# A two-layer float32 decoder trunk: six of eight MLP up-projection groups computed as 2x2 Strassen block products

## The chip, the core and the metric

The kernel runs on one core of a Trainium2 chip. The metric is the device time of one execution in microseconds (us). Five engines run their own instruction queues in order and wait for each other through semaphores: TensorE (PE in the profile, its weight loads as PEld), VectorE (DVE), ScalarE (ACT), GpSimd (POOL) and SyncE (SP), which here issues the DMA loads. Matmuls write PSUM, everything else lives in SBUF.

## The reference, cut to what matters

One sequence of 256 rows and 1024 columns goes through two layers. Each layer adds a normed mixer (retention in layer 0, block attention in layer 1) and then a normed MLP of width 4096:

```
def sq_relu_mlp(x, w_up, w_down):
    h = jax.nn.relu(x @ w_up)
    return (h * h) @ w_down
...
    h = h + rms_norm(mixers[i % N_MIXERS](rms_norm(h, pre), w_in, w_out), post)
    h = h + rms_norm(sq_relu_mlp(rms_norm(h, mpre), w_up, w_down), mpost)
```

All of it is float32. The change touches `x @ w_up` alone, 256 x 1024 times 1024 x 4096, once in each layer.

## The kernel before, in words

**Split products.** A float32 operand is split into two float32r parts, `hi` (a ScalarE copy) and `lo` (VectorE: operand minus `hi`). A product is three matmuls into one PSUM bank: hi*hi, hi*lo, lo*hi (`mm`, L178 to L180). The 256 rows are two row tiles of 128 (`t`); the 1024 inner columns are eight k tiles.

**Weight stream.** `Stream` brings weights as chunks of 128 x 1024 (512 KB). SP loads a chunk into one of four `raw` buffers, ScalarE writes `whi` (L134), VectorE `wlo` (L135). At most ten split chunks are live (`slots`); one is given back when its last matmul has been issued. `used` counts that down.

**Order of emission.** One Python program writes all queues. `Flow.now` is a clock that `mm` moves on by the planned time of its matmuls; side chains (generators such as `act_rows`) say after how much planned time they go on, and `pump` splits the next chunk when the planned time `next_t` has come and the chunk's load is planned to have landed. The order so made is the order in each engine's queue. On the chip nothing is reordered.

**The MLP** (`mlp`). The hidden width 4096 is eight groups of 512 columns.

- Groups 0 and 1 (`in_groups_skewed`): activations are the stationary operand, 512 weight columns the moving one. Row tile 0 of both groups comes first, then row tile 1. Each result goes through `act_rows`: ScalarE relu (`r`), VectorE square (`sq`), four TensorE transposes (`turn4`, tile `tp_u`), and a split of the transposed tile by ScalarE and VectorE into `hid[g]`.
- Groups 2 to 7 (`up_cols`): 128 weight columns are stationary and all 256 rows move, so results (`upc`) come out transposed and no `turn4` is needed. A group takes 4 column tiles x 8 k tiles x 3 = 96 matmuls of 256 columns. `act_cols` is relu, square, split.
- After each such group come four steps of the down projection (`step_out`, tile `dn`), each 2 row tiles x 2 column halves x 3 matmuls of 512 columns. In layer 1 the last of the four accumulators is kept as two tiles of 256 columns, so the end of the kernel can start on the first half (`finish_last`).

SP issues every load; GpSimd does only small work. In front of the MLP the function `post` finishes the mixer: norm, residual into `h`, transposition (`tp_h`), gain (`hg`), split, and a ScalarE pass over `h` for the next row norm (`pre_stats`).

Of the kernel before, what the change touches and what calls it, by code (L numbers as in the profile page):

```python
# [84 lines left out]
class Chunk:  # L85
    def __init__(self, hi, lo):
        self.hi, self.lo, self.left = hi, lo, CH * S


class Stream:  # L90
    """Weight chunks in the order of use: loaded, then split into two float32r parts."""

    def __init__(self, tc, ctx, flow, slots, raws):
        self.nc = tc.nc
        self.pool = ctx.enter_context(tc.tile_pool(name="wst", bufs=1))
        self.flow, self.slots, self.raws = flow, slots, raws
        self.src, self.raw, self.ready = [], [], []
        self.live, self.next_t, self.dma_t = 0, 0.0, 0.0
        flow.pump = self.pump

    def load(self):
        """issue the next chunk's load, and the other loads that come before it"""
        while self.src:
            s = self.src.pop(0)
            self.dma_t = max(self.dma_t, self.flow.now + 1.6)
            if callable(s):
                s()
                self.dma_t += 1.0
                continue
# [10 lines left out]
            return  # L120

    def split(self, pres=(None,)):
        nc = self.nc
        if not self.raw:
            self.load()
        raw = self.raw.pop(0)[0]
        hi = self.pool.tile([P, CH], F32R, tag="whi", name="whi", bufs=self.slots)
        lo = self.pool.tile([P, CH], F32R, tag="wlo", name="wlo", bufs=self.slots)
        n = len(pres)
# [7 lines left out]
        self.ready.append(Chunk(hi, lo))  # L137
        self.next_t = max(self.next_t, self.flow.now) + (1.3 if len(self.ready) < 4 else 2.0)
        while len(self.raw) < self.raws and self.src:
            self.load()  # L140

    def pump(self):
        while self.live < self.slots and self.flow.now >= self.next_t:
            if not self.raw:
                self.load()
            if not self.raw or self.flow.now < self.raw[0][1]:
                return
            self.split()
# [14 lines left out]
def body(ctx, tc, xT, x, gT, gpost, w_in_0, w_out_0, w_up_0, w_down_0, w_in_1, w_out_1, w_up_1, w_down_1,  # L163
# [12 lines left out]
    def mm(o, a, b, first, last):  # L176
        """o += a.T @ b; a, b: (hi, lo) pairs of float32r parts."""
        nc.tensor.matmul(o, a[0], b[0], start=first, stop=False)  # L178
        nc.tensor.matmul(o, a[0], b[1], start=False, stop=False)  # L179
        nc.tensor.matmul(o, a[1], b[0], start=False, stop=last)  # L180
        flow.now += 3 * b[0].shape[-1] / 2400

    def mm_rows(o, a, w, s, first, last):
        """activations stationary: o [128 rows, columns s of w]"""
        mm(o, a, (w.hi[:, s], w.lo[:, s]), first, last)
# [4 lines left out]
    def mm_cols(o, w, s, b, first, last):  # L190
        """weights stationary: o [128 columns s of w, all rows]"""
# [44 lines left out]
    h = [cpool.tile([P, D], F32, name=f"h{t}") for t in range(NT)]  # L236
    table = small_t("table")
    nc.scalar.activation(table, mhalf, AF.Copy)

    def rsqrt(ss):  # L240
        """(ss + eps) ** -0.5"""
# [6 lines left out]
    def pre_stats(t):  # L248
        """1 / rms of the rows of h[t]"""
# [4 lines left out]
    class HT:  # L254
        """h transposed, times the norm's gain, as two parts; its rows' 1 / rms come later."""
# [23 lines left out]
    class Post:  # L279
        """rms_norm of the rows z * sc, taken in parts as they come"""  # L280
# [8 lines left out]
        def part(self, z, c0):  # L289
            """the columns from c0"""  # L290
# [22 lines left out]
    def post(z, t, sc, gb, nxt, gi):  # L313
        """h[t] += rms_norm(z * sc) * gain; then h[t] transposed for the next layer."""
# [9 lines left out]
        hg = []  # L324
        for n in range(2):
            tp = new_ps([P, 4, P], "tp_h")
            turn4(tp, h[t][:, n * 512:(n + 1) * 512])
            hg.append(new_e2([P, 4, P], "hg"))
            gn = g_sb[:, gi, n * 4:n * 4 + 4]
            nc.vector.tensor_mul(hg[n], tp, gn[:, :, None].to_broadcast([P, 4, P]))  # L330
        yield 0.8
        for n in range(2):
            n4, ts = slice(n * 4, n * 4 + 4), slice(t * P, (t + 1) * P)
            split(nxt.hi[:, n4, ts], nxt.lo[:, n4, ts], hg[n])
# [11 lines left out]
    def finish_out(acc, lhs, k0, nk, sc, gb, nxt, gi):  # L346
        """the rest of an output projection and the norm after it, row tile 0 ahead of row tile 1"""
# [14 lines left out]
    def in_tile(hT, w, c, t, o):  # L362
        """two k tiles of one group of 512 columns"""
# [4 lines left out]
    def in_group_both(hT):  # L368
        """one group of 512 columns for both row tiles, chunk after chunk"""
# [7 lines left out]
    def in_groups_skewed(hT, then):  # L377
        """two groups of 512 columns, row tile 0 ahead of row tile 1"""
# [9 lines left out]
        hT.ready(1)  # L388
        for g in range(2):
# [6 lines left out]
    def mlp(hT, gain, nxt, gi):  # L396
# [18 lines left out]
        def act_cols(g, jp, o):  # L415
            r = new_e2([P, 2, S], "r")
            nc.scalar.activation(r, o, AF.Relu)  # L417
            sq = new_e2([P, 2, S], "sq")
            nc.vector.tensor_mul(sq, r, r)
            yield 0.8  # L420
            j2 = slice(jp * 2, jp * 2 + 2)
            split(hid[g][:, 0, j2, :], hid[g][:, 1, j2, :], sq)

        def up_cols(g):
            chunks = [ws.get() for _ in range(4)]
            for jp in range(2):
                o = new_ps([P, 2, S], "upc")
                for j in range(2):
                    f0 = (jp * 2 + j) * P
                    for k in range(KD):  # L430
                        s = slice((k % 2) * 512 + f0, (k % 2) * 512 + f0 + P)
                        mm_cols(o[:, j, :], chunks[k // 2], s, hT.both(k), k == 0, k == KD - 1)
                done[g].append(flow.spawn(act_cols(g, jp, o)))
# [8 lines left out]
        in_groups_skewed(hT, lambda g, t, o: done[g].append(flow.spawn(act_rows(g, t, o))))  # L442
# [10 lines left out]
        for g in range(2, NG):  # L453
            new_hid(g)
            up_cols(g)
            for k in range((g - 2) * 4, (g - 1) * 4):
                w = ws.get()
                for t in range(NT):
                    step_out(acc, lhs, k, t, w, nk)
# [55 lines left out]
    def load_h(t):  # L515
        return lambda: nc.sync.dma_start(h[t], x[t * P:(t + 1) * P, :])

    src = ws.src
    wi = [w_in_0[c] for c in range(48)]
    src += [(wi[0], (load_x(0, 1), load_x(1, 1))), (wi[1], (load_x(2, 2), None)), (wi[2], (load_x(4, 2), None)), load_x(6, 2),  # L520
            wi[3], wi[4], wi[5], wi[6], wi[7], load_h(0), load_h(1), lambda: nc.sync.dma_start(csr, cs0), wi[8],
            load_decay(0), wi[9], wi[10], wi[11]]
    for hd in range(1, RH):
        src += wi[hd * 12:hd * 12 + 6] + [load_decay(hd)] + wi[hd * 12 + 6:hd * 12 + 12]
        if hd == 1:
            src += [lambda: consts.update(gb=load_gain(0))]
    src += [w_out_0[k] for k in range(16)]

    def mlp_order(up, down):
        o = [up[c] for c in range(8)]  # L530
        for g in range(2, NG):
            o += [up[g * 4 + c] for c in range(4)]
            o += [down[(g - 2) * 4 + c] for c in range(4)]
        return o + [down[(NG - 2) * 4 + c] for c in range(8)]

    src += mlp_order(w_up_0, w_down_0)
    src += [w_in_1[g * 4 + c] for g in (0, 1, 3, 4, 2, 5) for c in range(4)]
    src += [w_out_1[k] for k in range(MH)]
    src += mlp_order(w_up_1, w_down_1)
# [9 lines left out]
    def qk_tile(o, i, c, w):  # L549
        """two k tiles of one of the four 128-column tiles of a head's q and k (even, odd)"""  # L550
# [4 lines left out]
    def first_stats():  # L555
        """1 / rms of the rows of x, also into the rotary tables"""
# [130 lines left out]
    hT = mlp(hT, 1, HT, 2)  # L687

# [11 lines left out]
    def prep(qk, u, t, ps, wait):  # L700
        """rotary and transposition of q or k of four heads, one row tile"""
# [24 lines left out]
    def softmax(qk, pall, hp, t, *after):  # L726
        """rows of softmax(q k.T) of two heads, one row tile; b is the weight of a key out of reach"""
# [34 lines left out]
    def turn(pall, pts, after):  # L762
        """the probabilities transposed, head after head"""
# [32 lines left out]
    def pts_of(a, b):  # L796
        """two tiles of 2048 columns -> the parts of four heads' transposed probabilities"""
# [17 lines left out]
    def heads0(qk, pq):  # L815
        """the first four heads: all that follows their q and k"""
# [11 lines left out]
    def heads1(qk, pq):  # L828
        """the last four heads, up to their transposed probabilities"""
# [43 lines left out]
    mlp(hT, 3, None, None)  # L873
# [4 lines left out]
def _groups(w, cols):  # L878
    """[K, N] -> chunks of [128, 2 x 512]: groups of 512 columns in the order cols, two k tiles a chunk"""
# [3 lines left out]
    return w.reshape(n * 4, P, CH)  # L883

# [63 lines left out]
```

## Time and profile before

| | us |
|---|---|
| device time, 3 runs: median (lowest to highest) | 690.31 (690.25 to 691.45) |
| profiled execution: span, first to last instruction | 688.4 |
| median run less that span (the profile gives no other total of its own) | 1.9 |
| PE busy, share of span | 676.1 (98%) |
| DVE busy, share | 419.4 (61%) |
| ACT busy, share | 350.4 (51%) |
| POOL busy, share | 82.2 (12%) |
[...]

Busy times are of instructions that overlap in a pipelined engine: the length of one matmul in the profile (0.39 us for 512 columns) is not the step between two matmuls. That step is read from two start times in the timeline. "Releaser" is the instruction that ended an engine's wait.

### The profile page before, as it was taken

To read this page: it belongs to the slowest core of one execution; us is meant where nothing else is said; L and a number is where in the kernel's file an instruction comes from. 1 tells how busy PE (TensorE), PEld (TensorE's weight loads), DVE (VectorE), ACT (ScalarE), POOL (GpSimd) and SP (SyncE) were. 2 spreads that over 40 slices of the span, in tenths; PEclk is the share of its full clock that TensorE was granted. 3 is DMA by queue.
4 is the path that set the end of the run, shared out by engine and by line. 5 is a ranking of instruction groups with operands and counts; after the bars stand their busy time and mean duration, and the time that the engine had idled before them with its cause. 6 is when DMAs were issued, how large, how long until landed. Compare 5 with 4: busy or idle time off the path is not lost. (4 is left out here: it accounts for less than half of the span.)

```text
span 688.4 us, 10014 instructions
## 1 busy us (share of the span) xinstructions
PE 676.1 (98%) x3919; PEld 594.3 (86%) x3919; DVE 419.4 (61%) x521; ACT 350.4 (51%) x493; POOL 82.2 (12%) x138
## 2 busy tenths in 40 slices
PE   8999999999999999999999999999999999999996
PEld 6889898988888988998898878888889999999985
DVE  5669576656458665545653867867686654465513
ACT  6475555445346545435542657755465554345411
POOL 0222120201001000000000263922010000000001
PEclk9999999999999999999999999999999999999998
DMA  7767565464624774457545456543246744674401
GB/s 274 284 208 267 200 212 177 155 206 154 241 93 157 241 251 169 157 190 244 176 140 175 169 184 219 184 148 123 83 161 235 258 155 151 211 231 148 164 9 62
DMA packets 36191, 125.09 MB, mean 182 GB/s; under 512 B 4272, under 2 KB 4784, under 8 KB 36144
## 3 DMA queue, kind: packets, MB, share of 16 engines
q1 hardware_dynamic: 36144, 124.45, 53.0%
q8 instruction: 31, 0.51, 0.3%
q14 instruction: 16, 0.13, 0.1%
HBM read 123.39 MB, written 1.05 MB: 181 GB/s over the span
## 5 line engine op out<-in xcount | busy, mean ns | idle before, releaser
L135 DVE TENSOR_TENSOR wlo<-raw,whi 128x1024 fp32r<-128x1024 f32 (+1 forms) x227 | 271.5, 1212 | 114.1 <-ACT whi L134 112.8
L134 ACT ACTIVATE whi<-raw 128x1024 fp32r<-128x1024 f32 (+1 forms) x227 | 231.1, 1042 | 86.9 <-DMA raw<-in_w_down 21.1
L178 PE MATMUL ip<-whi,act 128*128 128x512 f32 x288 | 114.2, 397 | 0.0
L179 PE MATMUL ip<-wlo,act 128*128 128x512 f32 x288 | 112.5, 391 | 0.2 <-DVE wlo L135 0.2
L180 PE MATMUL ip<-whi,act 128*128 128x512 f32 x288 | 112.4, 390 | 0.0
L178 PE MATMUL upc<-act,whi 128*128 128x256 f32 x384 | 108.8, 283 | 0.0
L180 PE MATMUL upc<-act,wlo 128*128 128x256 f32 x384 | 108.7, 283 | 0.0
L179 PE MATMUL upc<-act,whi 128*128 128x256 f32 x384 | 108.7, 283 | 0.0
L179 PE MATMUL dn<-wlo,act 128*128 128x512 f32 (+1 forms) x288 | 105.6, 367 | 0.0
L178 PE MATMUL dn<-whi,act 128*128 128x512 f32 (+1 forms) x288 | 105.6, 367 | 0.0
L180 PE MATMUL dn<-whi,act 128*128 128x512 f32 (+1 forms) x288 | 105.3, 366 | 0.0
L178 PEld LDWEIGHTS upc<-act,whi 128*128 128x128 f32 x384 | 73.7, 192 | 0.3
L179 PEld LDWEIGHTS upc<-act,whi 128*128 128x128 f32 x384 | 73.7, 192 | 0.3
L180 PEld LDWEIGHTS upc<-act,wlo 128*128 128x128 f32 x384 | 73.7, 192 | 0.0
L180 PEld LDWEIGHTS ip<-whi,act 128*128 128x128 f32 x288 | 54.1, 188 | 11.6
L179 PEld LDWEIGHTS ip<-wlo,act 128*128 128x128 f32 x288 | 54.2, 188 | 10.7 <-DVE wlo L135 0.7
L178 PEld LDWEIGHTS ip<-whi,act 128*128 128x128 f32 x288 | 54.2, 188 | 10.0
L178 PEld LDWEIGHTS dn<-whi,act 128*128 128x128 f32 x288 | 54.4, 189 | 8.9
L180 PEld LDWEIGHTS dn<-whi,act 128*128 128x128 f32 x288 | 54.2, 188 | 8.9
L179 PEld LDWEIGHTS dn<-wlo,act 128*128 128x128 f32 x288 | 54.4, 189 | 8.6
L310 POOL TENSOR_TENSOR po_c<-po_sum,mhalf 128x1 f32<-128x1 f32 x8 | 4.5, 563 | 379.4 <-DVE po_sum L298 379.4
L417 ACT ACTIVATE r<-upc 128x512 f32<-128x512 f32 x24 | 14.3, 597 | 60.8 <-PE upc L180 60.8
(156 smaller groups left out, 862.4 us busy)
## 6 DMA issues: line engine op xcount, KB each, us to landing
raw<-in_w_in SPq DMA_DIRECT2D x69, 512.0 KB, 3.9
raw<-in_w_up SPq DMA_DIRECT2D x64, 512.0 KB, 4.5
raw<-in_w_down SPq DMA_DIRECT2D x64, 512.0 KB, 4.1
raw<-in_w_out SPq DMA_DIRECT2D x24, 512.0 KB, 3.3
gb<-in_gpost SPq DMA_DIRECT2D x4, 512.0 KB, 5.4
raw<-in_w_in SPq DMA_DIRECT2D x6, 256.0 KB, 5.6
h<-in_x SPq DMA_DIRECT2D x2, 512.0 KB, 6.6
dT_sb<-in_dT SPq DMA_DIRECT2D x4, 256.0 KB, 4.8
```

The lines of the kernel that those rows point to most:

```text
L134: nc.scalar.activation(hi[:, c], raw[:, c], AF.Copy)
L135: nc.vector.tensor_sub(lo[:, c], raw[:, c], hi[:, c].bitcast(F32))
L178: nc.tensor.matmul(o, a[0], b[0], start=first, stop=False)
L179: nc.tensor.matmul(o, a[0], b[1], start=False, stop=False)
L180: nc.tensor.matmul(o, a[1], b[0], start=False, stop=last)
L310: nc.gpsimd.tensor_tensor(c, self.ss, mhalf, ALU.pow)
L417: nc.scalar.activation(r, o, AF.Relu)
```

## The change

Groups 2 to 7 are taken in three pairs in each layer. A pair's up projection is a 2 x 2 block product: rows halve into the two row tiles, the inner 1024 into even and odd k tiles (each 4 tiles of 128), the 1024 columns of the pair into its two groups. Seven products of blocks (Winograd's form of Strassen's scheme) take the place of eight. Each product is 4 k tiles x 3 matmuls of 512 columns with activations, or a sum of activation blocks, as the stationary operand. The products go into three PSUM tiles, `px`, `py`, `pz`, some of them accumulated on top of an earlier one.

- **Activation sums**, once per MLP (`block_sums`): four sums of blocks of `hg`, each then split; eight VectorE and four ScalarE instructions of 128 x 512. `hg` now stays in SBUF for that.
- **Weight sums.** The up weights of a pair are loaded into four `quad` tiles of 128 x 2048, each in two halves. Two block sums are VectorE adds in place (`u1`, `u2`; L187), two are accumulating DMAs from SBUF to SBUF that GpSimd issues (`u3`, `u4`; L191). A pair has four VectorE adds and four such DMAs, 512 KB each.
- **Chunks.** A pair now splits 14 half blocks instead of 8 chunks of up weights, beside 8 chunks of down weights as before. A half block is used by 6 matmuls of 512 columns.
- **Results.** `squared` adds the stored blocks on VectorE (`c`, with `u2`, `u3`, `p1` as helpers), then ScalarE does relu and square, and after 1.6 planned us `turned` issues four transposes on TensorE and a split. A pair has four of these.
- **Order.** `up_blocks` alternates one product and one down step. `down()` is one step of 12 + 12 matmuls.
- **Pace.** While the quads are open a split costs the plan 1.5 us, an add 1.1 us, an accumulating DMA 2.8 us of the queue and 7.0 us to land.
- Layer 1's last accumulator is one tile of 512 columns again.

```
+    def product(o, lhsT, first):
+            for half in range(2):
+                w = ws.get()
+                for kk in range(2):
+                    kp = 2 * half + kk
+                    mm_rows(o, lhsT(kp), w, slice(kk * 512, (kk + 1) * 512), first and kp == 0, kp == 3,
+                            not first)
...
+    def up_blocks(g, down):
+            x = new_ps([P, 512], "px")
+            product(x, quad(0, 0), True)
+            p1 = new_e2([P, 512], "p1")
+            nc.scalar.activation(p1, x, AF.Copy)
+            down()
+            flow.finish(*sums)
+            z = new_ps([P, 512], "pz")
+            product(z, hsum(0), True)
+            down()
+            y = new_ps([P, 512], "py")
+            product(y, hsum(1), True)
+            u2 = new_e2([P, 512], "u2")
+            nc.vector.tensor_add(u2, y, p1)
+            down()
+            product(y, hsum(2), False)
+            u3 = new_e2([P, 512], "u3")
+            nc.vector.tensor_add(u3, y, p1)
+            squared(g + 1, 1, z, u3, -1.0)
+            down()
+            product(x, quad(0, 1), False)
+            squared(g, 0, x)
+            down()
+            product(y, quad(1, 1), False)
+            squared(g, 1, y, p1)
+            down()
+            product(z, hsum(3), False)
+            squared(g + 1, 0, z, u2, -1.0)
+            down()
+            down()
...
+        def squared(g, t, o, add=None, sign=1.0):
+            c = new_e2([P, 512], "c")
+            if add is None:
+                nc.scalar.activation(c, o, AF.Relu, scale=sign)
+            else:
+                nc.vector.tensor_add(c, o, add)
+                nc.scalar.activation(c, c, AF.Relu, scale=sign)
+            nc.scalar.activation(c, c, AF.Square)
+            done[g].append(flow.spawn(turned(g, t, c)))
...
+                if name[1] in ("u1", "u2"):
+                    nc.vector.tensor_add(o, o, a)
+                    cost += 1.1
+                    self.landed[name] = 0.0
+                else:
+                    nc.gpsimd.dma_start(o, a, accum_op=ALU.add)
+                    self.dma_t = max(self.dma_t, self.flow.now) + 2.8
+                    self.landed[name] = self.flow.now + 7.0
...
-        if nxt is None:
-            acc[1] = [acc[1][0], acc[1][1][:, :256], new_ps([P, 256], "dn4")]
```

**Place 1: VectorE, start of layer 0's MLP.** `sq` is the square of a result of groups 0 and 1, `act<-tp_u` the split of a transposed one, `rs_a` the end of `post`. Before, between the square of (group 0, row tile 0) and that of (group 0, row tile 1):

```order
L408 TENSOR_TENSOR sq<-r 128x512
L135 TENSOR_TENSOR wlo<-raw,whi 128x1024
L198 TENSOR_TENSOR act<-hg,act 128x4x128 x2
L135 TENSOR_TENSOR wlo<-raw,whi 128x1024
L198 TENSOR_TENSOR act<-tp_u,act 128x4x128
L243 TENSOR_SCALAR rs_a<-pre_ss 128x1
L408 TENSOR_TENSOR sq<-r 128x512
L135 TENSOR_TENSOR wlo<-raw,whi 128x1024 x2
L198 TENSOR_TENSOR act<-tp_u,act 128x4x128
L135 TENSOR_TENSOR wlo<-raw,whi 128x1024
L408 TENSOR_TENSOR sq<-r 128x512
```

The last row is the square of (group 0, row tile 1). Now, up to the same square; after `rs_a` and ahead of these rows stand five more: a split of `quad_2029`, an add into it, the square of (group 1, row tile 0), a block sum, a split of `quad_2029`:

```order
L187 TENSOR_TENSOR quad_2029<-quad_2029,quad_2030 128x1024
L505 SCALAR_TENSOR_TENSOR hsum<-hsum,hg 128x512
L258 TENSOR_TENSOR s_lo<-hsum,s_hi 128x512
L258 TENSOR_TENSOR act<-tp_u,act 128x4x128
L508 TENSOR_TENSOR hsum<-hg 128x512
L258 TENSOR_TENSOR s_lo<-hsum,s_hi 128x512
L182 TENSOR_TENSOR wlo<-raw,whi 128x1024
L182 TENSOR_TENSOR wlo<-quad_2029,whi 128x1024
L187 TENSOR_TENSOR quad_2029<-quad_2029,quad_2031 128x1024
L511 SCALAR_TENSOR_TENSOR hsum<-hsum,hg 128x512
L258 TENSOR_TENSOR s_lo<-hsum,s_hi 128x512
L470 TENSOR_TENSOR sq<-r 128x512
```

Behind `rs_a` that square was the sixth instruction. It is now the seventeenth: four splits of chunks, three adds, four block sums, three splits of sums, the split of a turned block and the square of (group 1, row tile 0) stand ahead of it.

**Place 2: VectorE, second half of a pair.** Layer 0, the pair of groups 4 and 5, from the split of the pair's second turned block (`act<-tp_u`) to the last `c`. `quad_2032` is the first block of the next pair. Before, one whole group there:

```order
L135 TENSOR_TENSOR wlo<-raw,whi 128x1024
L419 TENSOR_TENSOR sq<-r 128x512
L135 TENSOR_TENSOR wlo<-raw,whi 128x1024
L198 TENSOR_TENSOR act<-sq,act 128x512
L135 TENSOR_TENSOR wlo<-raw,whi 128x1024 x6
L419 TENSOR_TENSOR sq<-r 128x512
L198 TENSOR_TENSOR act<-sq,act 128x512
```

Now:

```order
L258 TENSOR_TENSOR act<-tp_u,act 128x4x128
L182 TENSOR_TENSOR wlo<-raw,whi 128x1024
L182 TENSOR_TENSOR wlo<-quad_2032,whi 128x1024
L187 TENSOR_TENSOR quad_2032<-quad_2032,quad_2031 128x1024
L491 TENSOR_TENSOR c<-py,p_2665 128x512
L258 TENSOR_TENSOR act<-tp_u,act 128x4x128
L182 TENSOR_TENSOR wlo<-quad_2032,whi 128x1024
L187 TENSOR_TENSOR quad_2032<-quad_2032,quad_2031 128x1024
L182 TENSOR_TENSOR wlo<-raw,whi 128x1024
L491 TENSOR_TENSOR c<-pz,u_2747 128x512
```

Two rows of the next pair's first block stand directly in front of `c<-py`, three rows of splitting and adding in front of `c<-pz`.

**Place 3: TensorE, layer 0, groups 2 and 3, from the end of the third `py` product.** Before, a down step (`dn`) was followed by the next down step or by the next group, with no transposes; two steps meet like this:

```order
L178 MATMUL dn_2255<-whi_2212,act_2027 128x512
L179 MATMUL dn_2255<-wlo_2213,act_2027 128x512
L180 MATMUL dn_2255<-whi_2212,act_2027 128x512
L178 MATMUL dn_2252<-whi_2234,act_2027 128x512
L179 MATMUL dn_2252<-wlo_2235,act_2027 128x512
```

Now (each accumulator `dn_` has three matmuls):

```order
L240 MATMUL py_2376<-whi_2423,act_1669 128x512
L238 MATMUL dn_2274<-whi_2442,act_2036 128x512
L239 MATMUL dn_2274<-wlo_2443,act_2036 128x512
L240 MATMUL dn_2274<-whi_2442,act_2036 128x512
L238 MATMUL dn_2275<-whi_2442,act_2036 128x512
L239 MATMUL dn_2275<-wlo_2443,act_2036 128x512
L240 MATMUL dn_2275<-whi_2442,act_2036 128x512
L238 MATMUL dn_2276<-whi_2442,act_2036 128x512
L239 MATMUL dn_2276<-wlo_2443,act_2036 128x512
L240 MATMUL dn_2276<-whi_2442,act_2036 128x512
L262 MATMUL tp_u_2555<-ident_96,c_2542 128x128 x4
L238 MATMUL dn_2277<-whi_2442,act_2036 128x512
```

The four transposes of `c` stand nine matmuls behind the product whose result `c` holds. It is so in all six pairs, four times in each.

## Rows read from the trace of the kernel before

**Rows 1.** The page: busy time of the engines, TensorE's granted clock in 40 slices.
```profile
PE 676.1 (98%) x3919; PEld 594.3 (86%) x3919; DVE 419.4 (61%) x521; ACT 350.4 (51%) x493; POOL 82.2 (12%) x138
...
PEclk9999999999999999999999999999999999999998
```
**Rows 2.** Windows, layer 1: length, busy PE, PEld, DVE, ACT, POOL, clock, DMA, GB/s.
```profile
580.85:603.49 22.64, 22.64 (x158) 21.14 (x157) 12.21 (x13) 10.38 (x12) 0.00 (x0) 1.00 0.58 186
603.49:626.13 22.64, 22.64 (x158) 21.14 (x157) 12.22 (x13) 10.38 (x12) 0.00 (x0) 1.00 0.57 186
```
**Rows 3.** Timeline of TensorE, layer 0: start, length, line, tile; twelve matmuls apart each.
```profile
321.58 0.28 PE L178 MATMUL upc<-act,whi 128*128 128x256 f32 x1
323.02 0.28 PE L178 MATMUL upc<-act,whi 128*128 128x256 f32 x1
...
334.08 0.39 PE L178 MATMUL dn<-whi,act 128*128 128x512 f32 x1
336.80 0.39 PE L178 MATMUL dn<-whi,act 128*128 128x512 f32 x1
```
**Rows 4.** The chain that ended last: start, us, instruction (one turn of layer 1).
```profile
509.95 0.44 PE tp_u L202 x4
```
**Rows 5.** Timeline of TensorE, layer 1: two down steps, each from its first matmul.
```profile
583.47 0.40 PE L178 MATMUL dn<-whi,act 128*128 128x512 f32 x1
...
586.25 0.40 PE L178 MATMUL dn<-whi,act 128*128 128x512 f32 x1
```
**Rows 6.** Timeline of ScalarE, end of layer 1: squares of 512 and of 256 columns.
```profile
676.36 0.69 ACT L293 ACTIVATE junk<-dn,po_s 128x512 bf16<-128x512 f32 x1 [4.55 <-PE dn L180]
...
682.08 0.47 ACT L293 ACTIVATE junk<-dn,po_s 128x256 bf16<-128x256 f32 x1 [2.30 <-issue]
```
**Rows 7.** Groups by form: count, then busy us, mean ns, idle time before.
```profile
L135 DVE TENSOR_TENSOR wlo<-raw,whi 128x1024 fp32r<-128x1024 f32 x221 | 267.6, 1226 | 113.4 <-ACT whi L134 112.1
L134 ACT ACTIVATE whi<-raw 128x1024 fp32r<-128x1024 f32 x221 | 227.6, 1054 | 86.5 <-DMA raw<-in_w_down 21.1 <-PE upc L179 15.4 <-DMA raw<-in_w_up 15.4
...
L405 ACT ACTIVATE r<-ip 128x512 f32<-128x512 f32 x8 | 4.7, 592 | 5.6 <-PE ip L180 5.6
...
L739 DVE TENSOR_TENSOR sm<-sp,cm 128x512 f32<-128x512 f32 x4 | 2.7, 682 | 0.0
```
**Rows 8.** Timelines of VectorE and ScalarE: instructions back to back, merged by the view.
```profile
215.99 1.28 DVE L198 TENSOR_TENSOR act<-hg,act 128x512 fp32r<-128x512 f32 x2
...
584.27 3.49 DVE L135 TENSOR_TENSOR wlo<-raw,whi 128x1024 fp32r<-128x1024 f32 x3
...
582.91 2.95 ACT L134 ACTIVATE whi<-raw 128x1024 fp32r<-128x1024 f32 x3
```
**Rows 9.** Timelines at layer 0's MLP start: ScalarE's row statistics, TensorE's second and third turns.
```profile
217.84 1.05 ACT L251 ACTIVATE junk<-h 128x1024 bf16<-128x1024 f32 x1
218.79 0.19 ACT L251 ACTIVATION_READ_ACCUMULATOR junk<-h 128x1 f32 x1
...
222.63 0.60 PE L202 MATMUL tp_u<-ident,sq 128*128 128x128 f32 x4
...
228.56 0.60 PE L202 MATMUL tp_u<-ident,sq 128*128 128x128 f32 x4
```
**Rows 10.** Timelines: a result's way from ScalarE to VectorE and from TensorE to ScalarE.
```profile
218.88 0.59 ACT L405 ACTIVATE r<-ip 128x512 f32<-128x512 f32 x1
219.50 0.69 DVE L408 TENSOR_TENSOR sq<-r 128x512 f32<-128x512 f32 x1 [0.34 <-ACT r L405]
...
597.45 0.28 PE L180 MATMUL upc<-act,wlo 128*128 128x256 f32 x1
...
597.77 0.60 ACT L417 ACTIVATE r<-upc 128x512 f32<-128x512 f32 x1 [4.27 <-PE upc L180]
```
**Rows 11.** DMA issues: count, KB each, median us to landing.
```profile
raw<-in_w_up SPq DMA_DIRECT2D x64, 512.0 KB, 4.5
raw<-in_w_down SPq DMA_DIRECT2D x64, 512.0 KB, 4.1
```

More of the change, by code (lines that the diff above doesn't have):

```diff
@@ L119, in load, with loaded @@
             self.raw.append((raw, self.dma_t + 0.9))
-            return
+            return True
+        return False
+    def loaded(self):
+        op = self.order[0]
+        if op is None:
+            return self.raw[0][1] if self.raw else None
+        t = [self.landed.get(n) for n in op.needs]
+        return None if None in t else max(t)
     def split(self, pres=(None,)):
         nc = self.nc
-        if not self.raw:
-            self.load()
-        raw = self.raw.pop(0)[0]
+        while self.loaded() is None:
+            assert self.load()
+        op = self.order.pop(0)
         hi = self.pool.tile([P, CH], F32R, tag="whi", name="whi", bufs=self.slots)
         lo = self.pool.tile([P, CH], F32R, tag="wlo", name="wlo", bufs=self.slots)
+        full = len(self.ready) >= (6 if self.quads else 4)
+        if op is None:
+            raw = self.raw.pop(0)[0]
+            cost = (1.5 if self.quads else 2.0) if full else 1.2
+        else:
+            raw = self.quads[op.q][:, op.half, :]
+            cost = 1.5 if full else 1.2
         n = len(pres)
@@ L135, in split @@
             nc.vector.tensor_sub(lo[:, c], raw[:, c], hi[:, c].bitcast(F32))
-        self.live += 1
[L137 to L140, printed above, removed]
-    def pump(self):
[L143 to L146, printed above, removed]
+        if op is not None:
+            for q, add, name in op.sums:
+                o, a = self.quads[q][:, op.half, :], self.quads[add][:, op.half, :]
+                if name[1] in ("u1", "u2"):
[6 more added lines that the diff above has]
+                    self.landed[name] = self.flow.now + 7.0
+        self.live += 1
+        self.quad_ops += op is not None
+        self.ready.append(Chunk(hi, lo, CH * S if op is None else CH * P))
+        self.next_t = max(self.next_t, self.flow.now) + cost
+        while len(self.raw) < self.raws and self.load():
+            pass
+    def pump(self):
+        while self.order and self.live < self.slots and self.flow.now >= self.next_t:
+            while self.loaded() is None:
+                if not self.load():
+                    return
+            if self.flow.now < self.loaded():
                 return
@@ L375, in in_group_both, with in_groups_skewed @@
         return o
-    def in_groups_skewed(hT, then):
+    def in_groups_skewed(hT, then, ready=None):
         held = []
@@ L388, in in_groups_skewed @@
         hT.ready(1)
+        if ready:
+            ready()
         for g in range(2):
@@ L393, in in_groups_skewed, with mlp @@
             then(g, 1, o)
-    def mlp(hT, gain, nxt, gi):
+    def mlp(hT, gain, nxt, gi, qpool):
+        ws.open_quads([qpool.tile([P, 2, CH], F32, name=f"quad{i}") for i in range(4)])
         hid = [None] * NG
@@ L413, in act_rows, with turned @@
             split(hid[g][:, 0, :, ts], hid[g][:, 1, :, ts], tp)
[L415 to L419, printed above, removed]
-            yield 0.8
[L421 to L433, printed above, removed]
+        def turned(g, t, c):
+            yield 1.6
+            tp = new_ps([P, 4, P], "tp_u")
+            turn4(tp, c)
+            ts = slice(t * P, (t + 1) * P)
+            split(hid[g][:, 0, :, ts], hid[g][:, 1, :, ts], tp)
@@ L523, in body @@
     for hd in range(1, RH):
-        src += wi[hd * 12:hd * 12 + 6] + [load_decay(hd)] + wi[hd * 12 + 6:hd * 12 + 12]
+        ws.add(*wi[hd * 12:hd * 12 + 6], load_decay(hd), *wi[hd * 12 + 6:hd * 12 + 12])
         if hd == 1:
[L526 to L534, printed above, removed]
@@ L541, in start_k @@
+    add_mlp(w_up_0, w_down_0, 0)
+    ws.add(*[w_in_1[g * 4 + c] for g in (0, 1, 3, 4, 2, 5) for c in range(4)])
+    ws.add(*[w_out_1[k] for k in range(MH)])
+    add_mlp(w_up_1, w_down_1, 14 * ((NG - 2) // 2))
     def start_k(k):
@@ L930 @@
     for i in range(2):
[L931 removed]
+        arrays[f"w_up_{i}"] = _blocks(a[f"w_up_{i}"])
         for n in ("w_out", "w_down"):
```

140 lines of the change are left out of this document (108 added, 32 removed).

## The prediction

> **What bounds the kernel now.** I read the page first: TensorE is busy 98% of the span and its clock stands at the upper level but for the first and last slices [rows 1]. The windows come next. In the MLP stages TensorE is busy all 22.64 us of a group (96 up matmuls, four down steps), while VectorE has 12.2 and ScalarE 10.4 us of work and the DMA engines are busy 57 to 58% [rows 2]. So the time is the number of matmuls by their step, as long as nothing reaches TensorE late. The chain of waits agrees: it is TensorE's, with turns (four transposes) in it at 0.44 us each [rows 4]. A change here is worth the matmuls it takes out, less the time it makes TensorE wait. The second needs the queues.
>
> **Matmuls removed.** Twelve up matmuls of 256 columns take 323.02 - 321.58 = 1.44 us, 0.120 each; twelve of 512 columns take 2.72 us, 0.2267 each [rows 3]. A pair of groups now takes 2 x 96 x 0.120 = 23.04 us. Seven products of 12 matmuls are 84 x 0.2267 = 19.04 us. Saved: 4.0 us a pair, six pairs, **-24.0 us**.
>
> [...]
>
> **Turns added.** Before, groups 2 to 7 came out transposed. Now each pair has four turns: 24 x 0.44 [rows 4] = **+10.6 us**.
>
> **Layer 1's split accumulator goes.** A down step there takes 586.25 - 583.47 = 2.78 us [rows 5] against 2.72: 24 steps, 1.4 us. The last eight steps have 48 matmuls of 256 columns in row tile 1, 5.76 us, which become 24 x 0.2267 = 5.44. The end then squares 512 columns in place of 256: 0.69 against 0.47 us [rows 6]. Together **-1.5 us**. With nothing late the span would be 688.4 - 24.0 + 10.6 - 1.5 = 673.5.
>
> **VectorE's and ScalarE's durations.** Three splits back to back take 3.49 us, the last 1.23, so a step is 1.13 on VectorE; ScalarE's is 0.95; a 512-column VectorE instruction steps by 0.60 [rows 7, 8]. No row has an add of 128 x 1024. Its nearest row is the split's subtraction, also two SBUF operands: 1.13. Bounds: 0 (hidden in a wait) and two steps of 512, 1.2. A read from PSUM is 0.68 on VectorE, 0.60 on ScalarE [rows 7]. A result passes between engines in 0.03 to 0.04 us, and TensorE's result is ready 0.20 us after the step of its last 512-column matmul (0.39 - 0.2267 + 0.04) [rows 3, 10].
> By these a pair's VectorE work is 22 splits (24.9), 4 adds (4.5) and nine 512-column instructions (5.7): 35 us out of 42.6 us of TensorE work. It fits on average; the order decides.
>
> **Start of each MLP.** ScalarE's row statistics end at 218.98 [rows 9], as before, and only behind them stands the copy of the first quad half; VectorE's first split then starts at 220.05. The square of (group 0, row tile 1) is the seventeenth instruction from there (place 1): four chunk splits and three adds at 1.13, ten 512-column instructions at 0.60 to 0.68. Sum 14.1 us, so it ends at 234.2. TensorE stands in queue order before its turn, which it reached at 228.56 before [rows 9]; the turn at 222.63 now waits 0.4 us for the square behind the first add, so it arrives at 229.0. It waits 5.2 us, and behind it are the last matmuls of group 1 and the first product. 5.6 us a layer, **+11.3 us**. Bounds: 0 if the adds and block sums slip into waits that were there anyway, 8 if splits run at their mean length of 1.23.
>
> **The turns in a pair.** A turn stands nine matmuls, 2.04 us, behind its product (place 3), and TensorE can't pass it.
> - `c` from `z` and `u3`: 0.20 + two dependent VectorE sums (0.68 + 0.03, twice) + relu and square (0.63 each) = 2.88. Wait 0.85, without any queue.
> - `c` from `x`: 0.20 + 1.26 = 1.46. No wait.
> - `c` from `y`: by itself 2.17. But it stands behind others (place 2). Count from the end of the first `c`. VectorE's next split needs a ScalarE copy that is queued behind relu and square, so it starts at 2.25; a split, a turned block and two splits to 6.3; the next copy is behind relu and square of `x` and ends at 7.45; split, turned block, split to 10.5; first block of the next pair and its add, 12.8. `y` is ready at 11.2. `c` is 1.6 late: wait 1.7.
> - `c` from `z` and `u2`: behind it TensorE's turn, then on VectorE a turned block, split, add, split, to 20.3; `z` is ready at 18.8. Wait 1.65.
>
> 4.2 us a pair. In the third pair of a layer no next pair follows: splits of down weights stand there without adds, `c` is late by 0.5 and 1.0, and the waits are 0.85 + 0.6 + 1.1 = 2.55. Both layers: 2 x (4.2 + 4.2 + 2.55) = **+21.9 us**. Bounds: 5.1 (six times 0.85 alone) and 30 (with splits at 1.23 and copies at 1.05).
>
> **Accumulating DMAs**: 24, costed at nothing. No row shows one. Two groups move 16 loads in 45.3 us at 57.5% [rows 2], 1.63 us of all engines each. An accumulate costs at least one such transfer and at most four (two reads, two writes, twice the rate lost); with four in a pair that is 6.5 to 26 us on top of 26, in a pair of 46.8 us. I take two transfers, nearest to a row: 39 us, 83%, hidden. `u4` is the tighter: some ten us lie between its issue and its split, against 4.1 to 4.5 us for a load to land [rows 11]; a landing after more than ten would hold up every split behind it. The plan's 2.8 and 7.0 us are only its own.
>
> **Sum.** 688.4 - 15.0 + 11.3 + 21.9 = 706.6 us of span. With the 1.9 us between the span and the median of the runs, 708.5.
>
> **Rivals.**
> A. *The waits don't come.* VectorE has 7 us to spare in a pair and ScalarE more; if copies and adds slip into gaps that my reckoning puts in series, c is ready in time, and only the chain of 0.85 stays: 690.3 - 15.0 + 5.1 = 680.4. For it: 35 us of work in 42.6. Against: queues are in order, and `c<-py` has the next pair's add directly in front of it. 14%.
> B. *Half the waits.* The start costs 2.8 a layer, the queues half of theirs: 690.3 - 15.0 + 5.6 + 5.1 + 8.4 = 694.4. For it: adds below 1.13, or loads that let the order's gaps close. 12%.
> C. *The accumulating DMAs fill the DMA engines.* At four transfers each a pair needs 52 us of DMA against 46.8, and every pair waits 5.2 more, now for weights: 708.5 + 31 = 740; it begins to decide just above three transfers (45.6 us). [...] For it: 57% is used already, and an accumulate must read both operands. Against: two thirds of the rest would have to go. 12%.
>
> The forecast, between 698 and 718, has 62%. A change that doesn't do what it says is excluded by the queues: the products stand in them.
>
> **The numbers.** Time 708.5. The range 684 to 722 leaves out most of A below and most of C above, 2 in 10; the forecast's own range is 698 to 718. A measurement of this kernel can tell 0.2%, 1.4 us, from no change: faster means under 688.9 (A and a little of B, 0.15), the same 688.9 to 691.7 (0.05), slower the rest (0.80).
>
> **What would show it.** In the profile after: TensorE's busy share under 95% with its clock unchanged; product matmuls at steps of 0.227; before the third `tp_u` of each MLP a wait of about 5 us for `sq`, and in each pair three waits for `c`, near 0.8, 1.7 and 1.7, named to ScalarE's square. VectorE's adds at 1.1 to 1.2 us. Wrong, if TensorE waits mainly for `whi` or `wlo` with DMA as the releaser further back (C), or if the waits at `tp_u` sum below 15 us (A, B).

## The result, and the profile after

| | before | after |
|---|---|---|
| device time, median (lowest to highest) | 690.28 us (690.18 to 691.45), 4 runs | 719.57 us (718.07 to 720.3), 4 runs |
| profiled span | 688.4 us | 716.3 us |
| mean granted TensorE clock in it, as a share of full speed | 0.995 | 0.987 |

The ratio is 1.0418, 95% interval 1.0403 to 1.0433: the change makes the kernel 29.3 us slower. The forecast was 708.5, so its sign was right, and 11 us of the loss were not in its sum. 719.57 lies in the range of 684 to 722, but above the 698 to 718 of the likeliest case.

The page after, against [rows 1]: busy time, the granted clock in 40 slices, and a queue that did not exist before (packets, MB, share of the DMA engines).

```profile
PE 671.2 (94%) x3271; PEld 556.6 (78%) x3271; DVE 497.8 (69%) x600; ACT 404.7 (56%) x565; POOL 101.5 (14%) x162
...
PEclk9999999999999899999999999999998999999999
...
q0 software_dynamic: 3456, 12.58, 10.1%
```

TensorE is at 94%, under the 95% named as a sign. But its clock is not unchanged: two slices show 8, and its mean is 0.987 where it was 0.995. The waits of TensorE (waited for; us in total, times, longest):

```profile
PE tp_u L262 <- ACT c L493: 21.3, 18, 1.7
PE tp_u L262 <- DVE sq L470: 11.3, 4, 5.2
```

These are the sums of the two wait terms, 21.9 and 11.3 us. One by one, in TensorE's timeline of layer 0 (start, length, tile, wait in brackets): the second and third turn of the MLP, and the three late turns of the pair of groups 4 and 5.

```profile
224.24 0.63 PE L262 MATMUL tp_u<-ident,sq 128*128 128x128 f32 x4 [0.41 <-DVE sq L470]
235.59 1.09 PE L262 MATMUL tp_u<-ident,sq 128*128 128x128 f32 x4 [5.23 <-DVE sq L470]
...
309.66 0.66 PE L262 MATMUL tp_u<-ident,c 128*128 128x128 f32 x4 [0.79 <-ACT c L493]
...
323.45 0.66 PE L262 MATMUL tp_u<-ident,c 128*128 128x128 f32 x4 [1.72 <-ACT c L493]
...
331.32 0.66 PE L262 MATMUL tp_u<-ident,c 128*128 128x128 f32 x4 [1.74 <-ACT c L493]
```

Predicted were 0.4 and 5.2, then 0.85, 1.7 and 1.65. What the sum lacks stands right behind the 5.23. The same timeline from there, and the windows of both layers at that place (the clock is the third figure from the end):

```profile
236.90 0.63 PE L239 MATMUL ip<-wlo,act 128*128 128x512 f32 x1
237.32 0.63 PE L240 MATMUL ip<-whi,act 128*128 128x512 f32 x1
...
240.66 0.39 PE L240 MATMUL px<-whi,act 128*128 128x512 f32 x1
240.89 0.39 PE L238 MATMUL px<-whi,act 128*128 128x512 f32 x1
```

```profile
236.00:240.00 4.00, 4.00 (x13) 3.23 (x12) 3.97 (x5) 2.22 (x4) 0.00 (x0) 0.50 0.00 0
...
540.00:545.00 5.00, 3.31 (x10) 2.86 (x11) 4.97 (x7) 3.12 (x4) 0.00 (x0) 0.54 0.02 6
545.00:550.00 5.00, 5.00 (x19) 3.95 (x19) 4.24 (x5) 3.37 (x5) 1.13 (x2) 0.78 0.56 196
```

A matmul of 512 columns steps by 0.42 to 0.43 us there and by 0.23 a little later, where [rows 3] had 0.2267: the granted clock of the first window is 0.50, and before it fell TensorE stood for 5.2 us. Read from the steps, that costs 2.2 us in layer 0 and 2.7 us in layer 1.

A whole pair, from the same matmul of `px` to that of the next pair, against [rows 2]; then the add (its group by form) and the accumulating DMA (the list of DMA issues), which had no row before ([rows 7, 11] were their nearest).

```profile
293.52:341.15 47.63, 43.38 (x198) 35.12 (x197) 36.08 (x36) 28.97 (x37) 3.44 (x5) 1.00 0.75 222
```

```profile
L187 DVE TENSOR_TENSOR quad<-quad,quad 128x1024 f32<-128x1024 f32 x24 | 29.4, 1225 | 0.8
```

```profile
quad<-quad POOLq DMA_DIRECT2D x24, 512.0 KB, 5.2
```

The square of 512 columns that ends layer 1 is as long as the one of [rows 6], 0.69:

```profile
709.40 0.69 ACT L354 ACTIVATE junk<-dn,po_s 128x512 bf16<-128x512 f32 x1 [4.64 <-PE dn L240]
```

The pair takes 47.63 us; the prediction's terms give 19.04 + 8 x 2.72 + 4 x 0.44 + 4.2 = 46.8. VectorE has 36.1 us of work in it, ScalarE 29.0, and yet TensorE waits for both.

### The profile page after: what moved, and what is told of

It is laid out like the page before. It is cut to its first block, busy times and chain, and to the rows that moved or that the text cites. A ratio compares the mean times of both kernels' runs of the same rounds, so it can differ in the third digit from the quotient of the medians.

```text
span 716.3 us, 8920 instructions
## 1 busy us (share of the span) xinstructions
PE 671.2 (94%) x3271; PEld 556.6 (78%) x3271; DVE 497.8 (69%) x600; ACT 404.7 (56%) x565; POOL 101.5 (14%) x162
## 3 DMA queue, kind: packets, MB, share of 16 engines
q1 hardware_dynamic: 36000, 124.45, 49.7%
q0 software_dynamic: 3456, 12.58, 10.1%
HBM read 123.39 MB, written 1.05 MB: 174 GB/s over the span
## 4 chain that ended last, share of the span: by engine, by line
PE 67%; DVE 12%; ACT 8%; issue 6%; POOL 3%; DMA 2%; SPq 0%; DVEq 0%; POOLq 0%; ACTq 0%
PE ip L238 7%; PE ip L239 7%; PE ip L240 6%; DVE wlo L182 5%; PE dn L238 5%; PE dn L240 5%; PE dn L239 5%; PE out L240 3%; PE out L239 3%; PE out L238 3%; ACT whi L181 3%; PE qk L240 2%; PE qk L239 2%; PE qk L238 2%; ACT c L493 2%
## 5 line engine op out<-in xcount | busy, mean ns | idle before, releaser
L182 DVE TENSOR_TENSOR wlo<-raw,whi 128x1024 fp32r<-128x1024 f32 (+1 forms) x179 | 213.9, 1208 | 94.3 <-ACT whi L181 90.9
L181 ACT ACTIVATE whi<-raw 128x1024 fp32r<-128x1024 f32 (+1 forms) x179 | 182.2, 1037 | 34.5 <-DMA raw<-in_w_in 11.5
L182 DVE TENSOR_TENSOR wlo<-quad,whi 128x1024 fp32r<-128x1024 f32 x84 | 99.9, 1219 | 12.1 <-ACT whi L181 11.8
L238 PE MATMUL dn<-whi,act 128*128 128x512 f32 x256 | 102.0, 399 | 0.0
L240 PE MATMUL dn<-whi,act 128*128 128x512 f32 x256 | 99.8, 390 | 0.0
L239 PE MATMUL dn<-wlo,act 128*128 128x512 f32 x256 | 99.7, 389 | 0.0
L181 ACT ACTIVATE whi<-quad 128x1024 fp32r<-128x1024 f32 x84 | 86.4, 1052 | 21.5 <-DMA quad<-quad 10.2
L240 PEld LDWEIGHTS ip<-whi,act 128*128 128x128 f32 x288 | 54.6, 190 | 11.8
L191 POOL DMA_DIRECT2D quad<-quad x24 | 21.1, 880 | 221.7 <-DVE quad L187 145.5
L492 ACT ACTIVATE c<-c 128x512 f32<-128x512 f32 x18 | 11.3, 630 | 70.1 <-DVE c L491 70.1
L238 PE MATMUL qk<-act,whi 128*128 128x256 f32 x128 | 37.2, 290 | 1.7 <-ACT whi L181 1.7
L238 PE MATMUL out<-whi,act 128*128 128x512 f32 x96 | 37.8, 394 | 0.0
L240 PE MATMUL out<-whi,act 128*128 128x512 f32 x96 | 37.4, 390 | 0.0
L240 PE MATMUL qk<-act,wlo 128*128 128x256 f32 x128 | 37.1, 290 | 0.3 <-DVE wlo L182 0.2
```

Of the source, the lines that this page charges most:

```text
L191: nc.gpsimd.dma_start(o, a, accum_op=ALU.add)
L238: nc.tensor.matmul(o, a[0], b[0], start=first, stop=False, skip_group_check=again)
L239: nc.tensor.matmul(o, a[0], b[1], start=False, stop=False, skip_group_check=again)
L240: nc.tensor.matmul(o, a[1], b[0], start=False, stop=last, skip_group_check=again)
L492: nc.scalar.activation(c, c, AF.Relu, scale=sign)
```

## The experiments

Ratios are to the kernel before, run on the same chip as the experiment; the last column is (ratio - 1.0418) x 690.3.

| run | median us | ratio, 95% interval | against the changed kernel, us |
|---|---|---|---|
| e4_fill | 714.42 | 1.0336 [1.0321, 1.0352] | -5.7 |
| e1_turn_late | 710.17 | 1.0277 [1.0260, 1.0294] | -9.7 |
| e2_sums_late | 714.03 | 1.0331 [1.0311, 1.0351] | -6.0 |
| e3_both | 703.17 | 1.0171 [1.0156, 1.0187] | -17.1 |
| e6_no_accum | 718.39 | 1.0405 [1.0390, 1.0421] | -0.9 |
| e7_no_adds | 698.39 | 1.0112 [1.0097, 1.0127] | -21.1 |
| e9_fused_only | 707.68 | 1.0247 [1.0222, 1.0272] | -11.8 |
| e5_fused | 689.38 | 0.9975 [0.9958, 0.9993] | -30.6 |
| e8_best | 681.33 | 0.9864 [0.9847, 0.9880] | -38.2 |
| e10_sq_act | 679.76 | 0.9840 [0.9817, 0.9863] | -39.9 |

**Is the slow stretch the clock, and does it come of the wait? (e4_fill)**

```
+            if g == 0 and t == 1:
+                fill = new_ps([P, 512], "fill")
+                for i in range(21):
+                    nc.tensor.matmul(fill, hT.hi[:, 0, 0:P], hT.hi[:, 0:2, :], start=True, stop=True)
             tp = new_ps([P, 4, P], "tp_u")
             turn4(tp, sq)
```

> 21 matmuls of 512 columns whose result nobody reads (4.76 us at the full step) are put on TensorE right ahead of the turn of (group 0, row tile 1), so inside the 5.2-us wait; the wait for the square ends when it did. Theory (the granted clock falls to 0.50 behind this wait because TensorE stood idle in it, and that costs 2.2 us in layer 0 and 2.7 us in layer 1): the clock stays near 1.0 there and the time falls by 4 to 5 us, to about 715. Rival (the slow stretch behind the wait has another cause, weights that come late or the records): the matmuls behind the wait still take 0.43 us a step, and the time is 719.6 or a little more.

Measured: -5.7 us, though TensorE has 42 matmuls more. The fill, the turn behind it in the timeline, and the window:

```profile
230.76 4.92 PE L475 MATMUL fill<-act 128*128 128x512 f32 x21
236.14 0.63 PE L262 MATMUL tp_u<-ident,sq 128*128 128x128 f32 x4 [0.46 <-DVE sq L470]
```

```profile
236.00:240.00 4.00, 3.86 (x19) 3.30 (x20) 3.97 (x5) 3.60 (x6) 0.00 (x0) 1.00 0.00 0
```

The turn starts 5.4 us after the first fill matmul, as late as in the changed kernel, and the clock stands at 1.00. So the fall comes of TensorE standing still, not of the code behind, and it costs about 5 us in all: from the first turn to the last `dn` the two MLPs are 2.0 and 2.6 us shorter in the profile than in the changed kernel's, against 2.2 and 2.7 read from the steps.

**Order alone: turns later, sums later, both (e1_turn_late, e2_sums_late, e3_both)**

The first edit, in `turned`, is e1; the second, in `mlp`, is e2; e3 has both.

```
-            yield 1.6
+            yield 4.4
...
-                         lambda: sums.append(flow.spawn(block_sums(), 1.0)))
+                         lambda: sums.append(flow.spawn(block_sums(), 6.0)))
```

> The turn of each c stands 21 matmuls (4.76 us) behind its product instead of 9 (2.04 us). Theory (c is late because VectorE's and ScalarE's queues stand in front of it, by up to 1.9 us, and a later turn simply doesn't meet the lateness): the waits for c, 21.3 us in the changed kernel's row, fall under 3 us in all, and the 5.2-us waits at the start of each MLP stay; time 719.6 - 18 to 21 = 698 to 702. Rival (VectorE and ScalarE are the bound of a pair, so that the lateness only moves): TensorE then waits for weight splits instead, and the time stays within 5 us of 719.6.

> The four block sums and their splits (at the start of each MLP) are put into the queues behind the square of (group 0, row tile 1) instead of ahead of it; nothing else is changed. Theory (the 5.2-us wait is this square standing behind twelve instructions of block sums and adds, and the clock's fall to 0.50 behind it comes of the wait): the wait falls by about 4 us in each layer, to 1 or 2 us, the granted clock stays near 1.0 there, and the time falls by 8 (waits) + 5 (clock) = 13 us, to about 706. Rival 1 (the clock's fall has nothing to do with the wait): 8 us, to 711, with the clock still at 0.50 for some 4 us. Rival 2 (the sums come too late for the second product): TensorE waits for hsum instead, no gain.

> Both edits: turns 21 matmuls behind their products, block sums behind the square of (group 0, row tile 1). Theory (the waits are two separate sets, both of order alone): gains add up, 18 to 21 + 13 = 31 to 34 us, time 685 to 689, a little under the kernel before (690.3); with every wait gone the matmuls alone would give 690.3 - 15.0 + 1.7 = 677. Rival (VectorE, 497.8 us busy in 716, has no room for more): waits for weight splits take their place, time 700 or more.

All three went the right way by half of what was expected: -9.7, -6.0, -17.1. TensorE's waits in e1, the last turn of the pair of groups 4 and 5, and the window behind it:

```profile
PE tp_u L262 <- DVE sq L470: 11.3, 4, 5.3
PE tp_u L262 <- ACT c L493: 10.4, 6, 2.4
```

```profile
331.29 0.66 PE L262 MATMUL tp_u<-ident,c 128*128 128x128 f32 x4 [2.38 <-ACT c L493]
```

```profile
331.29:334.00 2.71, 2.71 (x11) 2.29 (x12) 1.75 (x2) 2.71 (x4) 0.00 (x0) 0.73 0.12 42
```

A turn 2.7 us later does away with twelve of the eighteen waits, but the last `c` of a pair is now 2.38 us late instead of 1.74: without the earlier waits TensorE gets there sooner, and the two engines do not. The clock falls behind three of the four waits of 2.38 us, to 0.73 in the window above. In e2 the wait is split in two:

```profile
232.15 0.63 PE L262 MATMUL tp_u<-ident,sq 128*128 128x128 f32 x4 [1.60 <-DVE sq L470]
...
240.49 1.09 PE L262 MATMUL tp_u<-ident,sq 128*128 128x128 f32 x4 [2.24 <-DVE sq L470]
```

The edit puts all but the first of the block sums behind the square of (group 0, row tile 1). There they stand ahead of that of (group 1, row tile 1), which I had not followed: 11.3 us of waits become 8.5, not 3. Behind the second of these waits the clock stays at 1.00 in layer 1 and falls again in layer 0 (0.72 from 240 to 246 us).

For the waits for `c`, "order alone" therefore fell. Of the rival of e1 and e3 one half came: VectorE's queue, with its waits for ScalarE, is the bound of a pair, and the lateness moves to the last `c`. Its sign did not come, since no wait for a weight split takes the place. A pair of e3, from last turn to last turn, and VectorE's wait for ScalarE's copies in it:

```profile
283.41:328.75 45.34, 42.96 (x196) 35.28 (x197) 35.90 (x35) 28.65 (x36) 3.50 (x4) 1.00 0.77 232
```

```profile
DVE wlo L182 <- ACT whi L181: 7.1, 4, 2.3
```

VectorE works for 35.9 us, waits 7.1 us for copies and 2.1 us for `py`, which is nearly all of the 45.3.

e3's VectorE timeline shows what is left (the line after each `c` is the split, with its wait):

```profile
317.17 0.68 DVE L491 TENSOR_TENSOR c<-py,p 128x512 f32<-128x512 f32 x1
320.16 1.23 DVE L182 TENSOR_TENSOR wlo<-quad,whi 128x1024 fp32r<-128x1024 f32 x1 [2.31 <-ACT whi L181]
...
326.69 0.68 DVE L491 TENSOR_TENSOR c<-pz,u 128x512 f32<-128x512 f32 x1
329.68 1.23 DVE L182 TENSOR_TENSOR wlo<-quad,whi 128x1024 fp32r<-128x1024 f32 x1 [2.31 <-ACT whi L181]
```

and ScalarE's the other half:

```profile
317.88 0.63 ACT L492 ACTIVATE c<-c 128x512 f32<-128x512 f32 x1 [2.28 <-DVE c L491]
318.55 0.63 ACT L493 ACTIVATE c<-c 128x512 f32<-128x512 f32 x1
319.08 1.04 ACT L181 ACTIVATE whi<-quad 128x1024 fp32r<-128x1024 f32 x1
```

ScalarE waits for VectorE's sum, then does relu, square and the copy; VectorE waits for that copy. Each stands still for the other three times in a pair, 7 us of VectorE. The prediction's walk has this step, but none of the theories of e1 to e3 made anything of it.

**Cutting that loop (e5_fused, on top of e3_both)**

```
                 nc.vector.tensor_add(c, o, add)
-                nc.scalar.activation(c, c, AF.Relu, scale=sign)
-            nc.scalar.activation(c, c, AF.Square)
+            if add is None:
+                nc.scalar.activation(c, c, AF.Square)
+            else:
+                nc.vector.scalar_tensor_tensor(c, c, 0.0, c, op0=ALU.max if sign > 0 else ALU.min, op1=ALU.mult)
```

> On top of e3_both: for the three c of a pair that are sums, ScalarE's relu and square (two instructions, 0.63 us each) become one VectorE instruction, max(c, 0) times c (or min, where the sign is negative), some 0.60 to 0.68 us. In e3_both's trace each of these c stops VectorE for 2.31 us: its next split waits for a ScalarE copy that is queued behind relu and square, which wait for VectorE's add. Theory (that ping-pong, not VectorE's amount of work, makes the last c of a pair 2.4 us late): the 2.31-us idles of VectorE go, the waits for c fall from 10.5 to under 2 us, and time falls from 703.2 by 8.5 (waits) + 3 (clock behind them) = to about 692, though VectorE gets 18 x 0.6 = 11 us more work. Rival (VectorE is full): the added 1.8 us a pair make c as late as before; 702 to 706.

Measured 689.38 (ten runs, 685.78 to 690.62), against the theory's 692: no wait for `c` is left in TensorE's list. VectorE's idle time for `whi`, first in e3_both, then in e5_fused:

```profile
DVE wlo L182 <- ACT whi L181: 101.1, 79, 4.2
```

```profile
DVE wlo L182 <- ACT whi L181: 67.6, 71, 4.2
```

VectorE has more to do and is done sooner.

**Adds, loop and DMAs one at a time, in the changed kernel (e7_no_adds, e9_fused_only, e6_no_accum)**

The first line goes in e7, the second in e6; e9 is the changed kernel with the edit of e5_fused alone.

```
-                    nc.vector.tensor_add(o, o, a)
...
-                    nc.gpsimd.dma_start(o, a, accum_op=ALU.add)
```

> The changed kernel without the 24 VectorE adds into the quads (so u1 and u2 are not formed and the output is not the reference's). Theory (each add stands for 1.14 us in a queue that the late squares wait in): the wait at the start of each MLP falls from 5.2 by four adds, 4.5 us, to under 1 us, and with it the clock's fall; in each of the four pairs that prepare a next one, the second and third waits for c fall from 1.72 and 1.74 to about 0.6, by the one add in front of each. Time 719.6 - 9 (starts) - 5 (clock) - 9 (pairs) = about 697. Rival (the queues are late because of ScalarE's copies, and the adds slip into VectorE's idle time): pairs unchanged, 705 or more.

> The changed kernel with the one edit of e5_fused (square on VectorE where c is a sum), turns and block sums where the change put them. Theory (the adds only make c late because each split behind a c also stands still for 2.31 us until ScalarE has done relu, square and a copy): the second and third wait of a pair go, the first falls from 0.80 to about 0.3 (0.2 + 3 x 0.72 us against 2.04), so 21.3 us of waits for c become 2 to 4; the starts stay at 5.2 and the clock falls there as before: 719.6 - 18 = about 702. Rival (the adds in VectorE's queue are enough by themselves): waits of about 1 us stay in each pair's second and third place, 709 or more.

> The changed kernel without its 24 accumulating DMAs (so u3 and u4 are not formed and the output is not the reference's). Theory (they are hidden: no matmul waits for them, and the 10% of the DMA engines that they take is free time): 719.6, within 1.5 us. Rival C of the prediction in a mild form (they delay loads and splits, and so c): 5 us or more faster.

The three turns of the pair of groups 4 and 5 in e7, then in e9:

```profile
302.50 0.66 PE L261 MATMUL tp_u<-ident,c 128*128 128x128 f32 x4 [0.80 <-ACT c L492]
315.03 0.66 PE L261 MATMUL tp_u<-ident,c 128*128 128x128 f32 x4 [0.47 <-ACT c L492]
...
321.64 0.66 PE L261 MATMUL tp_u<-ident,c 128*128 128x128 f32 x4 [0.48 <-ACT c L492]
```

```profile
308.11 0.63 PE L262 MATMUL tp_u<-ident,c 128*128 128x128 f32 x4 [0.29 <-DVE c L495]
321.26 0.66 PE L262 MATMUL tp_u<-ident,c 128*128 128x128 f32 x4 [1.15 <-DVE c L495]
328.62 0.63 PE L262 MATMUL tp_u<-ident,c 128*128 128x128 f32 x4 [1.24 <-DVE c L495]
```

The second and third waits of 1.7 us have two parts, which add up to slightly more than the whole. Without the adds 0.47 is left: the add in front is worth 1.25, one VectorE add. Without the loop 1.15 to 1.24 is left: the loop is worth about 0.55. For e9 that makes its theory wrong (702 expected, 707.68 measured): the add alone holds `c` up by 1.2 us. Its rival (709 or more) named the right waits. In the third pair of each layer, which prepares no next one, e9 has 0.29 and nothing more. e7 came near its theory, 698.39 against 697: the pairs as expected, the starts not quite, where a wait of 2.04 us is left in each layer instead of under 1, and the clock still falls behind the one in layer 1 (0.68 from 530 to 534 us). And e6 is the changed kernel within 0.9 us: the DMAs are hidden.

**The rest of the start (e8_best on top of e5_fused, e10_sq_act on top of e8_best)**

The first two edits are e8, the third comes with e10; the first and the third are in `act_rows`.

```
-            yield 3.0
+            yield 5.0
...
-                         lambda: sums.append(flow.spawn(block_sums(), 6.0)))
+                         lambda: sums.append(flow.spawn(block_sums(), 11.4)))
...
-            nc.vector.tensor_mul(sq, r, r)
+            nc.scalar.activation(sq, r, AF.Square)
```

> On top of e5_fused: the block sums start 11.4 planned us behind row tile 0 instead of 6.0, behind nearly all squares of groups 0 and 1, and the turns of groups 0 and 1 stand 5.0 planned us behind their squares instead of 3.0. Theory: the remaining waits for sq (8.6 us in e3_both) go too, and with them the clock's falls; e5_fused less 8 to 9 us, about 683, and 7 us faster than the kernel before. If all waits were gone the matmuls would give 677. Rival (VectorE is busy without a gap from 222 to 248 us at the start of each MLP in e3_both, so the work only comes later): waits for hsum or for the first products' weights take their place, no gain over e5_fused.

> On top of e8_best: the four squares of groups 0 and 1 go from VectorE to ScalarE (0.63 us each), since VectorE runs without a gap at the start of each MLP in e8_best and its only new wait is there (1.2 us of TensorE for u2, twice). Theory (VectorE's amount of work sets that wait): it falls from 1.2 to 0, as 4 x 0.60 us leave VectorE: 681.3 - 2.4 = 679. Rival (ScalarE's copies then come later and hold VectorE's splits): the same 681 within 1 us, with VectorE idle for whi in that stretch.

e8 measured 681.33 where 683 was expected, e10 679.76 where 679 was: both faster than the kernel before, by 1.4 and 1.6%. In e8 the waits for `sq` are gone from TensorE's list, so for them order alone was enough; its two edits were not tried apart. What is left of waits in the MLP, in e8 and in e10:

```profile
PE py L238 <- DVE u L548: 2.4, 2, 1.2
```

```profile
PE py L238 <- DVE u L548: 1.3, 2, 0.6
```

The wait fell by half, not to nothing, and the intervals of e8 and e10 overlap, so this last step is not settled. In e10 a pair's period is 43.0 us, 0.4 above the 42.6 of the prediction's terms without waits.

## Why the prediction came out as it did, step by step

- **Matmuls removed, Turns added, Layer 1's accumulator** (-15.0 net): borne out. The span with nothing late was put at 673.5; e10, nearly without waits, has 678.2. Of the difference 1.3 us is the wait above, 1.2 the turns (below) and 0.5 a longer end; 1.7 was not traced to a cause. A turn in e10 (the view merges its four transposes), the matmul behind it and the next:

```profile
257.41 0.60 PE L262 MATMUL tp_u<-ident,c 128*128 128x128 f32 x4
257.76 0.48 PE L238 MATMUL px<-whi,act 128*128 128x512 f32 x1
258.08 0.39 PE L239 MATMUL px<-wlo,act 128*128 128x512 f32 x1
258.31 0.40 PE L240 MATMUL px<-whi,act 128*128 128x512 f32 x1
```

  From the turn to the second matmul behind it are 0.67 us, 0.44 more than a step. The dozen steps that follow are 0.23 instead of 0.2267, so that a turn costs 0.46 to 0.50 us in all, about 1.2 us more over 24 than predicted.
- **Start of each MLP** (+11.3): the waits are 0.41 + 5.23 in each layer, 11.3 us. The count of seventeen instructions held. Its "5.6 us a layer" was mis-sized all the same, since it priced the wait at its own length: behind it TensorE ran at a clock of 0.50, which cost another 2.2 and 2.7 us. e4_fill gives that back, 5.7 us measured. This is the largest term that the sum lacks, and the sign "with its clock unchanged" was wrong with it. No row of before has a wait of TensorE of this length inside an MLP. But the last slice of its clock [rows 1] shows a fall, to 8, at the idle end (the first slice, which the prediction names beside it, reads 9). And the trace of before has the price, at the start of the kernel:

```profile
10.00:12.00 2.00, 2.00 (x11) 2.00 (x11) 2.00 (x5) 1.96 (x5) 0.00 (x0) 0.50 1.05 388
```

  Between 5.5 and 8.2 us TensorE had waited four times, 0.85 us at most; in this window its clock is 0.50, and matmuls of 256 columns step by 0.21 us where [rows 3] have 0.12. I used neither. The same 0.50 stands behind the 5.23-us wait of the changed kernel.
- **The turns in a pair** (+21.9): the three waits came at the places named, at 0.79, 1.72 and 1.74 for 0.85, 1.7 and 1.65, and the view's sum is 21.3. Measured from when TensorE would have begun the turn, not from the modelled end of the matmul before, the waits are 0.96, 1.88 and 1.90, which makes some 2.3 us more over both layers. The prediction reckoned from that point, so that its figures lie so near to the view's is in part luck. The mechanism, queues that stand in each other's way, was right; e7 and e9 split it into adds (1.25) and the loop between VectorE and ScalarE (0.55).
- **Accumulating DMAs** (nothing): right. 10.1% of 716.3 us over 24 is 3.0 us of all engines each, against the 3.26 taken, and e6_no_accum moves nothing beyond 0.9 us. The bounds of one and four transfers of 1.63 us were the author's estimate, and no run shows the reads, writes and rate they were counted from; measured, 3.0 us is 1.8 transfers. Rival C falls. It also took the accumulates to run on the engines of the loads, which no row of before shows; the page after counts them as 10.1% of the 16 engines, beside 49.7% for q1, the queue of the loads.
- **Rivals A and B** (680.4 and 694.4) rested on the adds slipping into gaps; in the order of the change they do not. A's time can be had, by another order together with the edit of e5_fused: e8_best and e10_sq_act.
- **The sum.** The span rose by 27.9 us, predicted were 18.2. Of the 9.7 missing, the clock is 4.9 by its steps, the longer waits 2.3, the turns 1.2, a longer tail behind the last `dn` 0.5. Of the 0.8 left, 0.6 is the waits at the starts, measured in the same way (0.57 + 5.39 a layer). The stages before and between the MLPs are no cause: measured between the first turns and the last `dn`, they came out 1.05 us longer and 1.3 us shorter. The other 1.4 of the 11.1 us: the median lies 3.3 us above the profiled span, not 1.9, since the profiled execution (718.07) was the shortest of the four.

## What to carry to other kernels

Before taking matmuls out of a TensorE-bound kernel, see whether the queues that feed it still arrive in time: here 15 us were saved and some 40 us of waits and slow matmuls behind them came with it, at 69% and 56% busy feeders. Where two in-order engines hand a result back and forth (add, then relu and square, then a copy, then a split) while the same two also prepare the next weights, try the whole chain on one of them, even the busier, and let TensorE consume it later: here the first was worth 13.5 us on top of the second (e5 against e3). Price a long wait of TensorE with the slow matmuls behind it (here 2.2 and 2.7 us behind 5.2), and follow every instruction moved past the next consumer too, as the sums of e2 show.

## What the runs showed of the hardware that was not expected

- The granted clock fell to 0.50 behind each 5.2-us wait of TensorE in the changed kernel and in e1 and e9, and stood at 1.00 where the wait was filled with matmuls (e4). Behind waits of 2.0 to 2.5 us it fell in some places and not in others: in e1 behind three of four, in e3 behind three of six, in e2, e5 and e7 behind one of two. In windows of 4 us its lowest was 0.73 to 0.76 there in e1, 0.59 to 0.70 in e3, 0.78 in e2, 0.57 in e5 and 0.68 in e7, and 1.00 behind the other waits. Where it did in e1, a pair took 46.9 us; pairs of e3 without it took 45.3. The window in e3 behind the same wait of 2.38 us as the one of e1 above:

```profile
328.75:332.00 3.25, 3.25 (x16) 2.75 (x17) 2.29 (x2) 3.25 (x4) 0.00 (x0) 1.00 0.11 42
```

  What decides between them was not tried.
- An accumulating DMA of 512 KB within SBUF cost 3.0 us of all 16 engines, near two of the 1.63-us loads [rows 2], landed in 5.2 us in the median and held GpSimd's queue for 0.88 us.
